# Whole weight pieces of two k pairs with joint extra sums, seven of eight pairs in the attention, and raw buffers handed out by stage

## The chip, the cores and the metric

The kernel runs on one core of a Trainium2 chip. The metric is the device time of one execution in microseconds (us). The core has a matmul engine (PE, with its weight loads shown as PEld), a vector engine (DVE), an activation engine (ACT), and SP, whose in-order queue issues the DMA transfers. Every engine takes its own instructions strictly in the order of the program.

## What is computed

Two layers on a sequence of 512 rows of 2048 numbers, both with RMS norms before and after and with shift, scale and gate from a conditioning vector. The first layer is an mLSTM with 8 heads, the second an attention with 16 heads whose keys and values come from one shared projection of the stream between the layers. All of it is float32.

```python
proj = h @ w_in                                   # mLSTM: queries/keys, values, two gates o and z
qk = silu(causal_conv(proj[..., :A_V0], ...))
ht = mlstm_chunkwise(heads(q), heads(k), heads(v), li, lf)
y = sigmoid(o) * rmsnorm(ht) * silu(z) @ w_out

kv = hkv @ kv_w                                   # shared keys and values
qz = h @ w_in                                     # attention: queries and gate
s = einsum(q, k) * scale + bias                   # chunk attends to itself and eight before it
y = einsum(softmax(s), v) * silu(z) @ w_out
x = x + gate * rmsnorm(y, g_post)                 # after each layer
```

## The kernel before

**Products.** Every operand is split in two parts, hi (rounded) and lo (the rest), and a product is three matmuls, hi by hi, lo by hi and hi by lo (`mm3`, through `mm`, L213). Weights are packed on the host in the order in which they are used (`stream`), and come as pieces of up to 128 x 1024 numbers. `wpiece` (L183 on) fetches one into a `raw` tile (L194, tile names wr), makes the extra sums if the piece has any (ws, L199 to L201), casts hi on ACT (wh, L179), subtracts lo on DVE (wl, L180), and splits the sums in the same way (wsh, wsl). `raw`, `hi` and `lo` have three buffers each in the pool `wp`.

**Two ways of multiplying.** `proj_s` makes two tiles of output columns together. Over a pair of k tiles it either does the ordinary products (`eight`: twelve matmuls of 512 columns) or a fast 2 x 2 scheme (`seven`: seven products, twenty-one matmuls of 256 columns), which needs sums of the weights (the ws tiles) and of the activations (`half_sums`, `three_sums`). `f` of the eight pairs go the fast way: 5 in heads 4 to 7 of the mLSTM, 6 to 8 in the keys, 6 in the attention. Its four sums stand in the PSUM tiles ps_d, ps_c, ps_a and ps_b and are combined by DVE.

**Order.** The tile scheduler places the instructions of each engine in one order at build time. Weights run ahead of the rest by a priority lead (`AHEAD`), and buffers decide how far. The stages are: adaLN and gates (to about 243 us), mLSTM heads 0 to 3, heads 4 to 7 (to about 1545), the first output product in rows (to about 1890; its first column group also reloads the stored gates as yr tiles through the raw buffers), the values' first half, the keys, the values' second half (to about 2240), the attention's heads (to about 2650), and the second output product. In both output products the last column group, and in the values the first half, runs as two halves of two row tiles each (`PAIRS`).

**Head 4.** At h == HALF the pools of the first half are closed, and the activation sums for the fast products (`head_sums`) are made there, five pairs of them.

**Attention.** A head's weights come in six pieces. In the middle of a head's projection, `mid` puts the mixing of the head before the last (ps_o, gated in L1021) and the scores and transposes of the last one (ps_s, ps_t) into PE's order. `fetch` loads a head's keys and values into one tile at the start of the head before.

**Residual.** `residual(m)` loads a row tile, adds the first layer's output and stores it; for rows 2 and 3 this stands at high priority, just ahead of the values.

Of the kernel before, what the change touches and what calls it, by code (L numbers as in the profile page):

```python
# [15 lines left out]
P = 128  # L16
# [16 lines left out]
AHEAD = 300  # L33

# [8 lines left out]
HEAD_PAIRS = 5  # L43
HALF = NH // 2
ATT_PAIRS = 6


def pair_pieces(f, step=1):


    sk, nk = list(range(f)), list(range(f, KT // 2))
    n = min(len(sk), len(nk))
    out = [([a], [b]) for a, b in zip(sk, nk)]
    out[1:1] = [([], nk[i : i + 2]) for i in range(n, len(nk), 2)]
    return out + [(sk[i : i + step], []) for i in range(n, len(sk), step)]


def stream():

    out = []  # L60

    def add(mat, kts, cs):
        out.append((mat, [(k, c, n) for k in kts for c, n in cs]))

    def tile_a(mat, col, kts=KT):
        for k in range(0, kts, 8):
# [6 lines left out]
    def tile_s(mat, c1, c2, f, step=1):  # L73
        for sk, nk in pair_pieces(f, step):
            blocks = [(2 * k + i, c, P) for i, c in ((0, c1), (0, c2), (1, c2), (1, c1)) for k in sk]
            out.append((mat, blocks + [(2 * k + i, c, P) for k in nk for i in range(2) for c in (c1, c2)]))

    for k0, k1 in BLOCKS:
        for k in range(k0, k1):
            add("a_w_in", [k], [(c, P) for c in LEAD])  # L80
        for c in LATER:
            add("a_w_in", range(k0, k1), [(c, P)])
    for h in range(NH):
        for c in (h * DK, V0 // 2 + h * DK):
            if 1 < h <= HALF:
                tile_a("a_w_in", c)
                tile_a("a_w_in", c + P)
            elif h > HALF:
                tile_s("a_w_in", c, c + P, HEAD_PAIRS)
        tile_b("a_w_in", V0 + h * DV)  # L90
        if h >= HALF:
            for i in range(4):
                tile_s("a_w_in", O0 + h * DV + i * P, Z0 + h * DV + i * P, HEAD_PAIRS)
        elif h:
            for c0 in (O0, Z0):
                for i in range(4):
                    tile_a("a_w_in", c0 + h * DV + i * P)
    tile_b("a_w_out", 0, 32)
    for _ in PAIRS:
        for g in range(1, 4):  # L100
            tile_b("a_w_out", g * 512, 32)
    for _ in PAIRS:
        for g in range(2):
            tile_b("kv_w", D + g * 512)
    for i in range(KT // 2):
        tile_s("kv_w", 2 * i * P, (2 * i + 1) * P, KEY_PAIRS[i], 2)
    for g in range(2, 4):
        tile_b("kv_w", D + g * 512)
    for h in range(BH):
        tile_s("b_w_in", h * P, D + h * P, ATT_PAIRS)  # L110
# [20 lines left out]
def hybrid_trunk(ctx, tc, xT, xN, c, adaT, cols, wst, wg, ext, kc, out):  # L131
# [50 lines left out]
    ahead = [0]  # L182

    def wpiece(mat, ns=0, pl=None, bufs=2):


        i, at = wpos
        m, blocks = order[i]
        assert m == mat
        n = sum(w for _, _, w in blocks)  # L190
        wpos[:] = i + 1, at + P * n
        with tc.high_priority(ahead[0]):
            raw = wp.tile([P, 1024], F32, tag="raw", name=f"wr{i}")[:, :n]
            nc.sync.dma_start(raw, wst[at : at + P * n].rearrange("(p n) -> p n", p=P))  # L194
            out = []
            if ns:
                w = ns * P
                t = pl.tile([P, 3 * w], F32, tag="ws", name=f"ws{i}", bufs=2)
                nc.vector.tensor_tensor(t[:, : 2 * w], raw[:, w : 3 * w], raw[:, : 2 * w], op=ALU.subtract)  # L199
                nc.vector.tensor_tensor(raw[:, w : 2 * w], t[:, w : 2 * w], raw[:, :w], op=ALU.add)  # L200
                nc.vector.tensor_tensor(t[:, 2 * w :], raw[:, 3 * w : 4 * w], raw[:, w : 2 * w], op=ALU.subtract)  # L201
# [3 lines left out]
            if ns:  # L205
                sh = pl.tile([P, 3 * w], F32R, tag="wsh", name=f"wsh{i}", bufs=bufs)
                sl = pl.tile([P, 3 * w], F32R, tag="wsl", name=f"wsl{i}", bufs=bufs)
                split(sh, sl, t)
                return hi, lo, sh, sl
        return hi, lo  # L210
# [9 lines left out]
    def proj(mat, xs, pss, nk, k0, k1, last, t0=0, t1=S, first=None):  # L220

        g = len(pss)
        for ka in range(k0, k1, nk):
            hi, lo = wpiece(mat)
# [9 lines left out]
    def proj_b(mat, xs, pss, ms=range(4), kts=KT, at={}, late=0):  # L234
# [3 lines left out]
        for k0 in range(0, kts, 2):  # L238
            if k0 in at:
                at[k0]()  # L240
            held.append((k0, *wpiece(mat)))
# [13 lines left out]
    def proj_s(mat, xs, ss, f, z1, z2, name, pl, bufs, at={}, step=1):  # L255
# [3 lines left out]
        pieces = pair_pieces(f, step)  # L259
        begun = set()  # L260
        h0, h1_ = slice(0, 256), slice(256, 512)
        for i, (sk, nk) in enumerate(pieces):
            if i in at:
                at[i]()
            ns = len(sk)
            parts = wpiece(mat, ns, pl, bufs)

            def acc(ps, cols, b, x, last):
                start = id(ps) not in begun
                begun.add(id(ps))  # L270
                hi, lo = parts[:2] if b >= 0 else parts[2:]
                w0 = (b if b >= 0 else b + 3 * ns) * P
                w = slice(w0, w0 + P)
                mm3(ps[:, cols], hi[:, w], lo[:, w], x[:, 0, :], x[:, 1, :], start, last)

            def eight():
                for m, k in enumerate(nk):
                    for j in range(2):
                        for t, ps in enumerate((A, B)):
                            acc(ps, slice(0, S), 4 * ns + 4 * m + 2 * j + t, xs[2 * k + j], False)  # L280

            def seven():
                end = i == len(pieces) - 1
                for ps, cols, b0, x, last in (
                    (D, h1_, ns, lambda k: ss[k][1], False),
                    (D, h0, 0, lambda k: xs[2 * k][:, :, h0], end),
                    (C, h0, -2 * ns, lambda k: ss[k][2], False),
                    (C, h1_, -3 * ns, lambda k: ss[k][0], end),
                    (A, h0, 3 * ns, lambda k: xs[2 * k + 1][:, :, h0], False),
                    (A, h1_, -ns, lambda k: xs[2 * k + 1][:, :, h1_], end),  # L290
                    (B, h0, 2 * ns, lambda k: ss[k][3], end),
                ):
                    if i == 0 and ps is B:
                        eight()
                    for j, k in enumerate(sk):
                        acc(ps, cols, b0 + j, x(k), last and j == ns - 1)
# [3 lines left out]
            seven()  # L300
# [60 lines left out]
    sp = st.enter_context(pool("start"))  # L361
# [100 lines left out]
    bp = mst.enter_context(pool("ada1", side="right"))  # L462
# [110 lines left out]
    def pair(c, name):  # L573
        z1, z2 = (acp.tile([P, 2, 256], F32, tag="so", name=f"{name}_{i}", bufs=6) for i in range(2))
        proj_s("a_w_in", h1, h1s, HEAD_PAIRS, z1, z2, name, hq, 2)
# [32 lines left out]
    for h in range(NH):  # L608
# [49 lines left out]
        if h == HALF:  # L658
            head_sums()
# [87 lines left out]
    rp = rst.enter_context(pool("rp", bufs=12, side="right"))  # L747
# [3 lines left out]
    def y_tile(k):  # L751
        while len(ys) <= k:
            h, q = divmod(len(ys) // 2, 2)
            with tc.high_priority(AHEAD):
                raw = wp.tile([P, 2, S], F32, tag="raw", name=f"yr{h}_{q}")
# [144 lines left out]
    with tc.high_priority(AHEAD):  # L900
        residual(2)
        residual(3)
    for pair, ms in enumerate(PAIRS):
        for g in range(2):
# [3 lines left out]
            values(g, ms, turn)  # L908
    rst.close()
    zst = ExitStack()  # L910
    zp = zst.enter_context(pool("zp", bufs=2, side="right"))
    for i in range(KT // 2):
# [4 lines left out]
        proj_s("kv_w", hkv, hs, ready, z[:, 0:2, :], z[:, 2:4, :], f"k{i}", zp, 2, at, 2)  # L917
# [9 lines left out]
    for k in range(0, KT, 2):  # L927
# [11 lines left out]
        for i in range(2):  # L939
            split(h2[k + i][:, 0, :], h2[k + i][:, 1, :], raw[i])  # L940
    zst.close()
# [4 lines left out]
    kv = []  # L946

    def fetch(h):
        t = kq.tile([P, 2, S], F32, tag="kv", name=f"kv{h}", bufs=3)
        nc.sync.dma_start(t[:, 0, :], ksc[h // 2][:, h % 2, :])  # L950
        nc.sync.dma_start(t[:, 1, :], vsc[h // 4][:, h % 4, :])
        kv.append(t)

    fetch(0)

    def queries(h, mid):

        if h < BH - 1:
            fetch(h + 1)
        z = at.tile([P, 4, 256], F32, tag="z", name=f"z{h}", bufs=2)  # L960
        proj_s("b_w_in", h2, h2s, ATT_PAIRS, z[:, 0:2, :], z[:, 2:4, :], f"z{h}", kq, 3, {3: mid})
# [7 lines left out]
        split(k[:, 0, :], k[:, 1, :], kv[h][:, 0, :])  # L969
        bias = at.tile([P, S], F32, tag="b", name=f"bias{h}", bufs=2)  # L970
# [5 lines left out]
    def weights(h, q0, q, k, bias):  # L976
# [3 lines left out]
        for i in range(4):  # L980
            n = P * (i + 1)
            ps = newa(f"ps_s{h}_{i}")
            if i == 0:
                mm(ps[:, :n], q0, kv[h][:, 0, :P], True, True)
# [12 lines left out]
    def flipped(h, pr):  # L997
# [14 lines left out]
        split(v[:, 0, :], v[:, 1, :], kv[h][:, 1, :384])  # L1012
        return pts, v

    def mixed(h, pts, v, sz):
# [4 lines left out]
        mm(ps[:, 384:], kv[h][:, 1, 384:], pts[3], False, True)  # L1020
# [122 lines left out]
```

## Time and profile before

| | |
|---|---|
| median of 3 runs | 2827.09 us (2824.44 to 2833.84) |
| the profiled execution | 2828.65 us, span 2826.9 us, mean clock of PE 0.997 |
| PE, PEld, DVE, ACT busy | 99%, 86%, 73%, 47% of the span |
| matmuls on PE | 15173 |
| weight loads (wr) | 466 of 512 KB, 138 of 256 KB, 16 of 384 KB |

The span is the stretch that the profiler covers; the profiled execution's own time is 1.75 us longer. Busy time on PE is not speed: matmuls overlap, and the length listed for one includes its tail. Idle time is given with what ended it, so a wait names its releaser. The granted clock is the share of full speed that PE was given.

### The profile page before, as it was taken

The numbers are of one execution on the slowest core, as the hardware profiler recorded it, in microseconds if no ns is written. First come the engines' busy times: TensorE is split into PE (matmuls) and PEld (weight loads), VectorE is DVE, ScalarE is ACT, GpSimd is POOL, SyncE is SP. The second block draws the span as 40 slices with busy tenths as digits, with TensorE's granted clock in tenths as the row PEclk, the third lists the DMA queues.
The fourth block names the chain that finished last, engine by engine and source line by source line (L and its number), as shares of the span: only waits on it lengthen the run. The fifth ranks groups of instructions, "written<-read, shape, count | busy, mean of one in ns | idle before, by whom it ended". The sixth has DMA issues, their size and how long they took to land.

```text
span 2826.9 us, 40577 instructions
## 1 busy us (share of the span) xinstructions
PE 2788.7 (99%) x15173; PEld 2417.6 (86%) x15173; DVE 2050.1 (73%) x3668; ACT 1337.0 (47%) x2040; POOL 0.2 (0%) x4
## 2 busy tenths in 40 slices
PE   7999999999999999999999999999999999999998
PEld 5787888888888989989888888888998899999887
DVE  7986978878688776766857445567985688888625
ACT  4234524234234554544635344468534466666523
POOL 0000000000000000000000000000000000000000
PEclk9999999999999999999999999999999999999999
DMA  8875687878774332332323656788535534334634
GB/s 296 300 256 179 230 313 237 298 237 282 263 245 136 98 125 85 105 105 97 116 86 135 217 198 212 251 264 283 176 130 186 157 120 128 118 126 124 222 110 171
DMA packets 184606, 524.09 MB, mean 185 GB/s; under 512 B 19620, under 2 KB 37060, under 8 KB 183896
## 3 DMA queue, kind: packets, MB, share of 16 engines
q1 hardware_dynamic: 184408, 521.49, 55.1%
q8 instruction: 119, 1.95, 0.3%
q14 instruction: 79, 0.65, 0.1%
HBM read 487.81 MB, written 38.85 MB: 186 GB/s over the span
## 4 chain that ended last, share of the span: by engine, by line
PE 89%; DVE 4%; DMA 3%; ACT 2%; issue 1%; SPq 0%; DVEq 0%; ACTq 0%
PE ps_y L213 17%; PE ps_v L213 10%; PE ps_o L213 6%; PE ps_z L213 5%; PE ps_azo L213 4%; PE ps_qk L213 4%; PE ps_az L213 4%; PE ps_kv L213 4%; PE ps_l L213 3%; PE ps_bzo L213 3%; PE ps_bz L213 3%; PE ps_dz L213 2%; PE ps_cz L213 2%; PE ps_s L213 2%; PE ps_czo L213 2%; PE ps_dzo L213 2%
## 5 line engine op out<-in xcount | busy, mean ns | idle before, releaser
L179 ACT CAST wh<-wr 128x1024 fp32r<-128x1024 f32 (+3 forms) x640 | 595.8, 932 | 833.3 <-PE ps_y L213 230.3
L180 DVE TENSOR_TENSOR wl<-wr,wh 128x1024 fp32r<-128x1024 f32 (+3 forms) x640 | 687.4, 1075 | 390.2 <-ACT wh L179 384.3
L213 PE MATMUL ps_y<-wh,y 128*128 128x512 f32 x1536 | 475.9, 390 | 0.0
L213 PEld LDWEIGHTS ps_y<-wh,y 128*128 128x128 f32 x1536 | 288.3, 188 | 59.3
L213 PE MATMUL ps_v<-wh,h 128*128 128x512 f32 x1024 | 321.7, 390 | 0.0
L179 ACT CAST wsh<-ws 128x384 fp32r<-128x384 f32 (+1 forms) x238 | 131.1, 551 | 356.3 <-issue 171.1
L213 PE MATMUL ps_y<-wl,y 128*128 128x512 f32 x768 | 299.3, 390 | 0.0
L180 DVE TENSOR_TENSOR wsl<-ws,wsh 128x384 fp32r<-128x384 f32 (+1 forms) x238 | 143.3, 603 | 154.1 <-ACT wsh L179 154.0
L213 PEld LDWEIGHTS ps_v<-wh,h 128*128 128x128 f32 x1024 | 192.3, 188 | 40.3 <-DVE zq L306 0.9
L213 PE MATMUL ps_v<-wl,h 128*128 128x512 f32 x512 | 199.9, 390 | 0.0
L370 DVE CUSTOM_DVE_ANT_0 ada<-ada,scB,cl 128x1024 f32<-128x1024 f32 x128 | 163.9, 1281 | 23.4 <-DMA ada<-in_adaT 23.2
L370 DVE CUSTOM_DVE_ANT_0 ada<-ada,scB,mod 128x1024 f32<-128x1024 f32 x128 | 164.0, 1281 | 21.6 <-DMA ada<-in_adaT 20.1
L213 PEld LDWEIGHTS ps_y<-wl,y 128*128 128x128 f32 x768 | 144.2, 188 | 29.9 <-DVE wl L180 0.5
L213 PE MATMUL ps_kv<-wh,hkv 128*128 128x512 f32 x512 | 160.6, 393 | 1.0 <-ACT wh L179 1.0
L199 DVE TENSOR_TENSOR ws<-wr 128x256 f32<-128x256 f32 (+1 forms) x238 | 106.1, 452 | 35.3 <-DMA wr<-in_wst 34.1
L213 PE MATMUL ps_qk<-h,wh 128*128 128x512 f32 x384 | 119.1, 390 | 0.0
L213 PE MATMUL ps_o<-h,wh 128*128 128x512 f32 x384 | 118.3, 389 | 0.0
L213 PE MATMUL ps_z<-h,wh 128*128 128x512 f32 x384 | 118.2, 389 | 0.0
L213 PEld LDWEIGHTS ps_kv<-wh,hkv 128*128 128x128 f32 x512 | 96.6, 189 | 21.1 <-ACT wh L179 1.4
L213 PEld LDWEIGHTS ps_v<-wl,h 128*128 128x128 f32 x512 | 96.2, 188 | 19.7 <-issue 0.9
L213 PE MATMUL ps_l<-h,wh 128*128 128x512 f32 x320 | 99.1, 391 | 2.5 <-ACT oz L456 2.0
L213 PE MATMUL ps_kv<-wl,hkv 128*128 128x512 f32 x256 | 100.6, 393 | 0.8 <-DVE wl L180 0.8
(385 smaller groups left out, 5865.3 us busy)
## 6 DMA issues: line engine op xcount, KB each, us to landing
wr<-in_wst SPq DMA_DIRECT2D x466, 512.0 KB, 4.0
ada<-in_adaT SPq DMA_DIRECT2D x256, 512.0 KB, 5.9
wr<-in_wst SPq DMA_DIRECT2D x138, 256.0 KB, 2.7
xt<-nsc SPq DMA_DIRECT2D x44, 256.0 KB, 4.1
yr<-ysc SPq DMA_DIRECT2D x16, 512.0 KB, 4.3
wr<-in_wst SPq DMA_DIRECT2D x16, 384.0 KB, 5.4
bsc<-in_ext SPq DMA_DIRECT2D x16, 320.0 KB, 5.7
xt<-in_xT SPq DMA_DIRECT2D x4, 1024.0 KB, 7.1
```

What stands on the lines that cost most here:

```text
L179: nc.scalar.copy(hi, src)
L180: nc.vector.tensor_tensor(lo, src, hi.bitcast(F32), op=ALU.subtract)
L199: nc.vector.tensor_tensor(t[:, : 2 * w], raw[:, w : 3 * w], raw[:, : 2 * w], op=ALU.subtract)
L213: nc.tensor.matmul(ps, a, b, start=start, stop=stop)
L370: pin(nc.vector.tensor_tensor_reduce(at, at, scB[:, j * D // 2 : (j + 1) * D // 2], 1.0, mod[:, i : i + 1] if j else col(CB + i), ALU.mult ...
```

## The change

1. `raw` tiles: the pool `wp` keeps two instead of three buffers (`RAW_BUFS`). A third, for each third piece, is lent by a pool of the stage (`spare`): at the start, in heads 0 to 3, in the first output product's pool `rp` (used through the first half of the values), and in the keys. In heads 4 to 7, in the second half of the values, in the attention and in the second output product there is none. Of the reloaded y2r tiles, the first two use `wp`, the others a pool of their own.
2. `pair_pieces`: a piece with extra sums is always whole. Those that hold two fast pairs have either joint sums (`merged`, in keys and attention: sums of 512, 256, 256 columns and a split of 768) or two separate sets (heads 4 to 7).
3. The attention makes 7 of 8 pairs the fast way. A head has four pieces of 1024; `mid` stands before the third one. The split sums wsh and wsl have two buffers instead of three. Keys and values have tiles of their own, fetched in `mid`; the bias tile has one buffer instead of two.
4. Head 4's first column pair makes 4 pairs the fast way (`RAMP`), and the fifth pair's activation sums are made at its second piece.
5. `residual(2)` and `residual(3)` lose their high priority.

Over the kernel, PE gets 315 more matmuls of 256 columns and 180 fewer of 512, and SP issues 54 fewer loads for the same bytes.

```diff
+RAW_BUFS = 2
+RAMP = [4, 5, 5, 5]
-ATT_PAIRS = 6
-def pair_pieces(f, step=1):
+ATT_PAIRS = 7
+def pair_pieces(f, merged=False):
     sk, nk = list(range(f)), list(range(f, KT // 2))
-    n = min(len(sk), len(nk))
-    out = [([a], [b]) for a, b in zip(sk, nk)]
-    out[1:1] = [([], nk[i : i + 2]) for i in range(n, len(nk), 2)]
-    return out + [(sk[i : i + step], []) for i in range(n, len(sk), step)]
+    n = len(nk)
+    assert n <= f
+    out = [([[a]], [b]) for a, b in zip(sk, nk)]
+    return out + [([sk[i : i + 2]] if merged else [[k] for k in sk[i : i + 2]], []) for i in range(n, f, 2)]
...
-    def wpiece(mat, ns=0, pl=None, bufs=2):
+    def wpiece(mat, groups=(), pl=None, bufs=(2, 2)):
...
-            raw = wp.tile([P, 1024], F32, tag="raw", name=f"wr{i}")[:, :n]
+            own = spare[0] and i % (RAW_BUFS + 1) == 0
+            raw = (spare[0] if own else wp).tile([P, 1024], F32, tag="raw", name=f"wr{i}", bufs=1 if own else RAW_BUFS)[:, :n]
...
-            if ns:
+            for j, ns in enumerate(groups):
                 w = ns * P
...
-    sp = st.enter_context(pool("start"))
+    sp = spare[0] = st.enter_context(pool("start"))
...
-    bp = mst.enter_context(pool("ada1", side="right"))
+    bp = spare[0] = mst.enter_context(pool("ada1", side="right"))
...
             while loaded or pending:
                 background(3)
+            spare[0] = None
             mst.close()
...
-        if h == HALF:
-            head_sums()
...
-                o, sz = pair_oz = pair(O0 + h * DV + i * P, f"zo{h}_{i}")
+                f = HEAD_PAIRS if h > HALF else RAMP[i]
+                o, sz = pair(O0 + h * DV + i * P, f"zo{h}_{i}", f, {1: head_sums} if len(h1s) == f < HEAD_PAIRS else {})
...
-    rp = rst.enter_context(pool("rp", bufs=12, side="right"))
+    rp = spare[0] = rst.enter_context(pool("rp", bufs=12, side="right"))
...
-    with tc.high_priority(AHEAD):
-        residual(2)
-        residual(3)
+    residual(2)
+    residual(3)
...
+    spare[0] = None
     rst.close()
...
-        proj_s("kv_w", hkv, hs, ready, z[:, 0:2, :], z[:, 2:4, :], f"k{i}", zp, 2, at, 2)
+        spare[0] = zp
+        proj_s("kv_w", hkv, hs, ready, z[:, 0:2, :], z[:, 2:4, :], f"k{i}", zp, (2, 2), at, True)
...
-        proj_s("b_w_in", h2, h2s, ATT_PAIRS, z[:, 0:2, :], z[:, 2:4, :], f"z{h}", kq, 3, {3: mid})
+        proj_s("b_w_in", h2, h2s, ATT_PAIRS, z[:, 0:2, :], z[:, 2:4, :], f"z{h}", kq, (2, 2), {2: mid}, True)
...
-        bias = at.tile([P, S], F32, tag="b", name=f"bias{h}", bufs=2)
+        bias = at.tile([P, S], F32, tag="b", name=f"bias{h}")
...
             if 0 < h <= BH:
                 pr.extend(weights(h - 1, *qs.pop(h - 1)))
+            if h < BH - 1:
+                fetch_k(h + 1)
+            if h < BH:
+                fetch_v(h)
...
-            raw = wp.tile([P, 2, S], F32, tag="raw", name=f"y2r{i}")
+            raw = wp.tile([P, 2, S], F32, tag="raw", name=f"y2r{i}", bufs=RAW_BUFS) if i < 2 else op.tile([P, 2, S], F32, tag="yr", name=f"y2r{i}", bufs=2)
```

More of the change, by code (lines that the diff above doesn't have):

```diff
@@ L71, in tile_b, with tile_s @@
             add(mat, [k, k + 1], [(col, 512)])
-    def tile_s(mat, c1, c2, f, step=1):
-        for sk, nk in pair_pieces(f, step):
-            blocks = [(2 * k + i, c, P) for i, c in ((0, c1), (0, c2), (1, c2), (1, c1)) for k in sk]
+    def tile_s(mat, c1, c2, f, merged=False):
+        for sk, nk in pair_pieces(f, merged):
+            blocks = [(2 * k + i, c, P) for ks in sk for i, c in ((0, c1), (0, c2), (1, c2), (1, c1)) for k in ks]
             out.append((mat, blocks + [(2 * k + i, c, P) for k in nk for i in range(2) for c in (c1, c2)]))
@@ L92, in stream @@
             for i in range(4):
-                tile_s("a_w_in", O0 + h * DV + i * P, Z0 + h * DV + i * P, HEAD_PAIRS)
+                tile_s("a_w_in", O0 + h * DV + i * P, Z0 + h * DV + i * P, HEAD_PAIRS if h > HALF else RAMP[i])
         elif h:
@@ L182, in hybrid_trunk @@
     ahead = [0]
-    def wpiece(mat, ns=0, pl=None, bufs=2):
+    spare = [None]
+    def wpiece(mat, groups=(), pl=None, bufs=(2, 2)):
         i, at = wpos
@@ L192, in wpiece @@
         with tc.high_priority(ahead[0]):
-            raw = wp.tile([P, 1024], F32, tag="raw", name=f"wr{i}")[:, :n]
+            own = spare[0] and i % (RAW_BUFS + 1) == 0
+            raw = (spare[0] if own else wp).tile([P, 1024], F32, tag="raw", name=f"wr{i}", bufs=1 if own else RAW_BUFS)[:, :n]
             nc.sync.dma_start(raw, wst[at : at + P * n].rearrange("(p n) -> p n", p=P))
-            out = []
-            if ns:
+            ts = []
+            c0 = 0
+            for j, ns in enumerate(groups):
                 w = ns * P
[L198 to L201, printed above, removed]
+                r = raw[:, c0 : c0 + 4 * w]
+                t = pl.tile([P, 3 * w], F32, tag="ws", name=f"ws{i}_{j}", bufs=bufs[0])
+                nc.vector.tensor_tensor(t[:, : 2 * w], r[:, w : 3 * w], r[:, : 2 * w], op=ALU.subtract)
+                nc.vector.tensor_tensor(r[:, w : 2 * w], t[:, w : 2 * w], r[:, :w], op=ALU.add)
+                nc.vector.tensor_tensor(t[:, 2 * w :], r[:, 3 * w :], r[:, w : 2 * w], op=ALU.subtract)
+                ts.append(t)
+                c0 += 4 * w
             hi = wp.tile([P, 1024], F32R, tag="hi", name=f"wh{i}")[:, :n]
@@ L204, in wpiece @@
             split(hi, lo, raw)
-            if ns:
-                sh = pl.tile([P, 3 * w], F32R, tag="wsh", name=f"wsh{i}", bufs=bufs)
-                sl = pl.tile([P, 3 * w], F32R, tag="wsl", name=f"wsl{i}", bufs=bufs)
+            out = [(hi, lo)]
+            for j, t in enumerate(ts):
+                sh = pl.tile(list(t.shape), F32R, tag="wsh", name=f"wsh{i}_{j}", bufs=bufs[1])
+                sl = pl.tile(list(t.shape), F32R, tag="wsl", name=f"wsl{i}_{j}", bufs=bufs[1])
                 split(sh, sl, t)
-                return hi, lo, sh, sl
-        return hi, lo
+                out.append((sh, sl))
+        return out
     def mm(ps, a, b, start, stop):
@@ L253, in proj_b, with proj_s @@
             held.clear()
-    def proj_s(mat, xs, ss, f, z1, z2, name, pl, bufs, at={}, step=1):
+    def proj_s(mat, xs, ss, f, z1, z2, name, pl, bufs, at={}, merged=False):
         D, C, A, B = [newp(f"ps_{n}{name}") for n in "dcab"]
-        pieces = pair_pieces(f, step)
+        pieces = pair_pieces(f, merged)
         begun = set()
@@ L264, in proj_s, with acc @@
                 at[i]()
-            ns = len(sk)
-            parts = wpiece(mat, ns, pl, bufs)
-            def acc(ps, cols, b, x, last):
+            main, *extra = wpiece(mat, [len(ks) for ks in sk], pl, bufs)
+            def acc(ps, cols, parts, b, x, last):
                 start = id(ps) not in begun
                 begun.add(id(ps))
[L271 to L274, printed above, removed]
+                w = slice(b * P, (b + 1) * P)
+                mm3(ps[:, cols], parts[0][:, w], parts[1][:, w], x[:, 0, :], x[:, 1, :], start, last)
             def eight():
+                b0 = 4 * sum(len(ks) for ks in sk)
                 for m, k in enumerate(nk):
@@ L279, in eight, with seven @@
                         for t, ps in enumerate((A, B)):
[L280 to L291, printed above, removed]
+                            acc(ps, slice(0, S), main, b0 + 4 * m + 2 * j + t, xs[2 * k + j], False)
+            def seven(g, ks):
+                ns = len(ks)
+                b0 = 4 * sum(len(u) for u in sk[:g])
+                end = i == len(pieces) - 1 and g == len(sk) - 1
+                for ps, cols, t, at_, x, last in (
+                    (D, h1_, 0, 1, lambda k: ss[k][1], False),
+                    (D, h0, 0, 0, lambda k: xs[2 * k][:, :, h0], end),
+                    (C, h0, 1, 1, lambda k: ss[k][2], False),
+                    (C, h1_, 1, 0, lambda k: ss[k][0], end),
+                    (A, h0, 0, 3, lambda k: xs[2 * k + 1][:, :, h0], False),
+                    (A, h1_, 1, 2, lambda k: xs[2 * k + 1][:, :, h1_], end),
+                    (B, h0, 0, 2, lambda k: ss[k][3], end),
                 ):
-                    if i == 0 and ps is B:
+                    if i == 0 and g == 0 and ps is B:
                         eight()
-                    for j, k in enumerate(sk):
-                        acc(ps, cols, b0 + j, x(k), last and j == ns - 1)
+                    for j, k in enumerate(ks):
+                        acc(ps, cols, extra[g] if t else main, (0 if t else b0) + at_ * ns + j, x(k), last and j == ns - 1)
             if i:
                 eight()
-            seven()
+            for g, ks in enumerate(sk):
+                seven(g, ks)
         with tc.high_priority(AHEAD):
@@ L754, in y_tile @@
             with tc.high_priority(AHEAD):
-                raw = wp.tile([P, 2, S], F32, tag="raw", name=f"yr{h}_{q}")
+                raw = wp.tile([P, 2, S], F32, tag="raw", name=f"yr{h}_{q}", bufs=RAW_BUFS)
                 nc.sync.dma_start(raw, ysc[h, :, 2 * q : 2 * q + 2, :])
@@ L940, in hybrid_trunk @@
             split(h2[k + i][:, 0, :], h2[k + i][:, 1, :], raw[i])
+    spare[0] = None
     zst.close()
@@ L945, in hybrid_trunk, with fetch, fetch_k, fetch_v @@
     at = ast.enter_context(pool("att"))
[L946 to L954, printed above, removed]
+    kt, vt = [], []
+    def fetch(h, ts, src, tag):
+        ts.append(at.tile([P, S], F32, tag=tag, name=f"{tag}{h}", bufs=2))
+        nc.sync.dma_start(ts[h], src)
+    def fetch_k(h):
+        fetch(h, kt, ksc[h // 2][:, h % 2, :], "kt")
+    def fetch_v(h):
+        fetch(h, vt, vsc[h // 4][:, h % 4, :], "vt")
+    fetch_k(0)
     def queries(h, mid):
-        if h < BH - 1:
-            fetch(h + 1)
         z = at.tile([P, 4, 256], F32, tag="z", name=f"z{h}", bufs=2)
-        proj_s("b_w_in", h2, h2s, ATT_PAIRS, z[:, 0:2, :], z[:, 2:4, :], f"z{h}", kq, 3, {3: mid})
+        proj_s("b_w_in", h2, h2s, ATT_PAIRS, z[:, 0:2, :], z[:, 2:4, :], f"z{h}", kq, (2, 2), {2: mid}, True)
         qz = z.rearrange("p a t -> p (a t)")
@@ L968, in queries @@
         k = at.tile([P, 2, S], F32R, tag="kk", name=f"k{h}")
[L969 to L970 removed]
+        split(k[:, 0, :], k[:, 1, :], kt[h])
+        bias = at.tile([P, S], F32, tag="b", name=f"bias{h}")
         b0 = bsc[h]
@@ L1011, in flipped @@
         v = at.tile([P, 2, 384], F32R, tag="vv", name=f"vv{h}")
-        split(v[:, 0, :], v[:, 1, :], kv[h][:, 1, :384])
+        split(v[:, 0, :], v[:, 1, :], vt[h][:, :384])
         return pts, v
```

16 lines of the change are left out of this document (8 added, 8 removed).

## Prediction

> **What bounds the kernel now.** I read the page first, then the waits of the matmul engine, then single stages. The page gives the shares and the chain of work that ended last:
> ```profile
> PE 2788.7 (99%) x15173; PEld 2417.6 (86%) x15173; DVE 2050.1 (73%) x3668; ACT 1337.0 (47%) x2040; POOL 0.2 (0%) x4
> PE 89%; DVE 4%; DMA 3%; ACT 2%; issue 1%; SPq 0%; DVEq 0%; ACTq 0%
> ```
> PE is busy for 99% of the span. A gain can therefore come from cheaper products or from the few stops of PE, and from nothing else. The stops between 100 and 2810 us, longest first (waiter, what ended the wait, us, times, longest):
> ```profile
> PE ps_dzo L213 <- ACT wh L179: 3.7, 1, 3.7
> PE ps_kv L213 <- ACT wh L179: 1.0, 1, 1.0
> ...
> PE ps_kv L213 <- DVE wl L180: 0.8, 1, 0.8
> ```
> The first is at 895, where head 4 begins its joint columns; the others are at 1904, early in the values. Busy time and granted clock around them, and in a steady stretch of the attention:
> ```profile
> 895.00:900.00 5.00, 1.27 (x5) 1.14 (x5) 5.00 (x11) 3.68 (x6) 0.00 (x0) 0.72 0.16 52
> 900.00:905.00 5.00, 5.00 (x21) 4.43 (x20) 3.49 (x9) 1.51 (x3) 0.00 (x0) 0.59 0.30 108
> 1905.00:1910.00 5.00, 3.35 (x9) 2.42 (x10) 2.61 (x4) 2.75 (x4) 0.00 (x0) 0.76 0.82 251
> 2400.00:2450.00 50.00, 49.97 (x357) 46.77 (x356) 43.08 (x117) 32.42 (x63) 0.00 (x0) 1.00 0.39 123
> ```
> After the length come PE, PEld, DVE, ACT and POOL, then the clock, DMA share and GB/s. A stop costs its idle time and then a low clock: 0.59 over 900 to 905 is 5 x 0.41 = 2.05 us more, so the first stop costs 5.8 us. The stop at 1904 shows 0.76 after only 1.74 us of idleness; I put its low clock at 0.8 us on top, 2.5 us in all. By the Trainium skill, page "TensorE: Matmul & The Clock Gate", Part 1, the clock falls only after an idle window of about 3.4 us; by that rule the second stop would cost 1.7 us. The first stop agrees with the rule, the 0.76 at the second does not, and the row is used. In the attention nothing is free: PE 49.97 of 50, DVE 43.08, so heads cost what PE costs, with DVE not far behind.
>
> **Products.** One k pair of an attention head, ordinary and then fast, in the timeline of PE (start, length, tile):
> ```profile
> 2408.33 0.63 PE L213 MATMUL ps_az<-h,wh 128*128 128x512 f32 x2
> ...
> 2411.08 0.40 PE L213 MATMUL ps_bz<-h2s,wh 128*128 128x256 f32 x2
> ...
> 2414.57 0.40 PE L213 MATMUL ps_dz<-h2s,wh 128*128 128x256 f32 x2
> ...
> 2417.08 0.40 PE L213 MATMUL ps_dz<-h2s,wh 128*128 128x256 f32 x2
> ```
> Twelve 512-wide matmuls take 2411.08 - 2408.33 = 2.75 us, twenty-one 256-wide ones 2417.08 - 2414.57 = 2.51 us. Listed lengths (0.28 to 0.39) contain a tail that overlaps, so starts are the price. A pair turned from ordinary to fast saves 0.24 us. Sixteen heads get one more fast pair and the first column pair of head 4 one fewer: 15 x 0.24 = **-3.6 us**. The same page of the Trainium skill (Part 1, on the 2.5 ns) has N / 2.4 GHz + 2.5 ns a matmul, as an estimate 0.295 us a pair and -4.4 us; the trace is slower on both widths (0.229 and 0.120 us), so its row is used.
>
> **Joint pieces and extra sums.** The attention's weights come as four full pieces a head instead of two full and four half ones. Prices on DVE, from the groups by form in 2350 to 2600 (line, tile, shape, busy, mean ns):
> ```profile
> L180 DVE TENSOR_TENSOR wsl<-ws,wsh 128x384 fp32r<-128x384 f32 x60 | 33.3, 555 | 20.9 <-ACT wsh L179 20.9
> L180 DVE TENSOR_TENSOR wl<-wr,wh 128x512 fp32r<-128x512 f32 x40 | 27.5, 688 | 0.0
> L199 DVE TENSOR_TENSOR ws<-wr 128x256 f32<-128x256 f32 x59 | 24.6, 417 | 0.5 <-DMA wr<-in_wst 0.5
> L180 DVE TENSOR_TENSOR wl<-wr,wh 128x1024 fp32r<-128x1024 f32 x20 | 24.4, 1222 | 7.1 <-ACT wh L179 7.1
> ```
> Before, a head needs 6 x (0.417 + 0.285 + 0.288 + 0.555) + 4 x 0.688 + 2 x 1.222 = 14.5 us of weight work on DVE. After: one piece with a single pair, 1.545 + 1.222 = 2.8, and three joint pieces of 512, 256, 256 and 768 columns; I price those 0.69, 0.42, 0.42 and 0.96 by the slope of the rows, 3.7 us with the 1.22, so 13.9 in all. DVE and ACT lie under PE, so this brings no time by itself; 54 fewer issues of 0.33 us on SP bring none either, as the bytes are the same. Keys and values fetched apart, in the middle of a head, add one DMA queue step per head before the weights' loads: nothing while loads lead by a piece. The bias has one buffer instead of two, so its load waits until the last scores have read it; the weights behind it in SP's queue wait longer for their own buffer, so that adds nothing.
>
> The room for the attention's split sums falls from three to two. DVE takes its instructions in order, so a subtraction of sums that waits for room holds what is queued behind it: the gate product that reads ps_o (L1021) and frees PE's third score tile. I walked one head by these durations. From the head's first matmul, the room comes free at 9.4 us, its subtraction ends at 11.2, that of the fourth piece at 12.5, the first sum of the next head at 13.1, the gate product at 13.8; PE wants the bank at about 14.1. A margin of 0.3 us is within what the walk can tell, so I charge 0.06 us a head, **+1.0 us** (0 to +5).
>
> **Head 4.** One pair's activation sums leave the front. From the weights' subtraction at 873.05 to v's first, DVE then has 4 x 1.14 + 14 x 0.60 + 6 x 0.47 + 17 x 0.334 + 7 x 0.205 = 22.9 us in its queue (1024, 512, 384, 256, 128 columns, start to start), while PE has 893.44 - 873.05 = 20.4 us and 0.7 more before it needs the first split sums: still 1.8 us late, and by the same count 1.0 us at the next tile. What is late next is again DVE. 2.8 us of idleness instead of 3.7, in two shorter stops: **-1.5 us** (0, if the clock falls as much, to -5.8, if both vanish).
>
> **Values.** At 1904 the weights of the values stand in SP's queue behind the row loads and stores of the last residual rows, which now lose their precedence. Weights go first: **-2.5 us** (0 to -3.4, with the whole clock deficit of 1905 to 1915).
>
> **Two raw buffers instead of three.** Where a spare is lent (rows in halves, first values, keys) there are three as before. In heads 4 to 7 and in the attention PE spends at least 5 us on a piece, and two buffers deliver one per 3 to 3.5 us; that is hidden. In the output rows of the first layer five loads pass for three pieces of 5.45 us, 16.35 us of PE against 5 x 3.3 = 16.5 us: hidden by the lead of several us at its start, with little left. The last column group of the second output product is different: 16 pieces, each for two row tiles. In ACT's timeline, PE releases one cast after another there:
> ```profile
> 2776.42 1.05 ACT L179 CAST wh<-wr 128x1024 fp32r<-128x1024 f32 x1 [1.02 <-PE ps_y L213]
> 2779.14 1.05 ACT L179 CAST wh<-wr 128x1024 fp32r<-128x1024 f32 x1 [1.67 <-PE ps_y L213]
> ```
> In DVE's, the subtraction that frees the raw buffer of the first of them; and in the raw tile's own group, from 2745 on, the landing:
> ```profile
> 2777.51 1.23 DVE L180 TENSOR_TENSOR wl<-wr,wh 128x1024 fp32r<-128x1024 f32 x1 [1.45 <-ACT wh L179]
> ```
> ```profile
> DMA to landing us min/median/max: 3.1/3.4/5.4
> ```
> PE eats a piece per 2.72 us. A raw buffer is taken for 3.4 (landing) + 2.3 (cast to the end of the subtraction) + 0.2 (handovers) = 5.9 to 6.0 us, so two give a piece per 3.0 us. Counted from 2773.7, where the group starts, piece 4 is issued at 2.4 and piece 5 at 5.1; six periods later 14 and 15 are ready at 38.3 and 41.0, or 43 with the last landing of 5.4. Their use is at 36.7 and 38.1. The early lead covers the rest, the end does not: **+4.0 us** (0 to +6).
>
> Sum: -3.6 + 1.0 - 1.5 - 2.5 + 4.0 = -2.6 us. The profiled execution took 2828.65 us (1.75 around the span), so 2826.0; it stands 1.56 above the median of the runs, so about 2824.5. About 0.3%, 8.5 us, is what a measurement of this kernel tells from no change; the forecast is within it.
>
> **Rivals.** First, the stops go and nothing new comes: -3.6 - 5.8 - 3.4 = -12.8, or 2814. For it: each of these stops is named by the change. Against: DVE is full from 880 to 895, and the last group's arithmetic. Chance 0.2.
>
> Second, slower: two raw buffers throttle the attention. The first sum of the next head's second piece stands in DVE's queue right ahead of the gate product; its load can start only when the piece two before it is split, at 8.0 us of the head, and DVE wants it at 12.5. It decides above a landing of about 4.4 us. The page has 4.0 for such loads, the end of the kernel up to 5.4, and each us over the mark stops PE in all 16 heads: at 5.4, 16 us, or 2840. Against: DMA is at 0.39 here. Chance 0.25.
>
> Third, the products save nothing, because weight loads bind as in the key stage, where every product is 256 wide and PEld is busy for all of the time: the sum is +1.0, about 2828. Against: the 0.120 us above are just as large there. Chance 0.1.
>
> **Numbers.** Forecast 0.45 at 2824.5, rivals 0.2, 0.25 and 0.1. Faster by over 0.3% comes from the first rival, 0.2; slower from the second and a little of the forecast's own tail, 0.28; the rest is 0.52. The range takes in the first rival and the second almost to its full price: 2813 to 2839.
>
> **What would show it.** Right: about 25.2 instead of 25.4 us from one ps_o to the next; a shorter stop at ps_czo near 893; no stop at ps_kv near 1904; 3 to 5 us of waits of ps_y for wh or wl after 2800. Wrong: repeated waits of ps_s for L1036's product or of ps_t in the attention, casts that wait for wr there, stops of ps_y in the 1515 to 1700 stretch, or an end without waits.

## The result, and the profile after

The changed kernel takes 2833.47 us in the median of 12 runs, the kernel before 2825.98 in the same runs. The ratio is 1.0026, with a 95% interval of 1.0017 to 1.0035: 7.5 us slower, where the sum had 2.6 us faster. The time lies inside the stated range, on the other side of no change.

The page's shares and the chain that ended last:

```profile
PE 2788.1 (98%) x15308; PEld 2421.5 (85%) x15308; DVE 2057.1 (73%) x3488; ACT 1333.3 (47%) x1957; POOL 0.2 (0%) x4
PE 85%; DVE 7%; DMA 4%; ACT 2%; issue 2%; SPq 0%; DVEq 0%; ACTq 0%
```

PE is as busy as before, in a longer span; DVE has a larger part of the chain. The five longest waits of PE between 100 and 2815 us (waiter, what ended the wait, us, times, longest):

```profile
PE ps_czo L223 <- DVE v L182: 3.0, 1, 3.0
PE ps_t L1018 <- DVE pt L182: 2.7, 5, 1.1
PE ps_y L223 <- ACT wh L181: 2.3, 1, 2.3
PE ps_s L223 <- DVE e L605: 1.1, 1, 1.1
PE ps_azo L223 <- DVE v L182: 1.0, 1, 1.0
```

The two stops of ps_kv are gone. In place of one stop of 3.7 us at head 4 there are two of 3.0 and 1.0. New are five waits of ps_t in the attention, and a stop of ps_y at 2811. The windows with the clock:

```profile
1905.00:1910.00 5.00, 5.00 (x24) 4.14 (x23) 3.64 (x4) 3.62 (x7) 0.00 (x0) 1.00 0.99 333
2400.00:2450.00 50.00, 49.75 (x376) 47.62 (x375) 43.80 (x100) 32.23 (x55) 0.00 (x0) 1.00 0.38 127
2815.00:2820.00 5.00, 5.00 (x16) 4.01 (x17) 1.23 (x1) 1.04 (x1) 0.00 (x0) 0.67 0.02 9
```

1904 is now at full clock; 2815 to 2820, behind the new stop, is at 0.67.

A ledger shows where the time went. It takes the start of the first matmul of a tile in PE's timeline, and compares the length from one such start to the next, so that early differences don't carry on:

| stretch, from the first matmul of ... to ... | before | after | difference |
|---|---|---|---|
| start to ps_dzo (head 4) | 893.44 | 894.32 | +0.9 |
| ps_dzo to ps_y (heads 4 to 7) | 638.94 | 637.42 | -1.5 |
| ps_y to ps_kv (first output rows) | 356.05 | 356.45 | +0.4 |
| ps_kv to ps_dk (values) | 94.95 | 91.15 | -3.8 |
| ps_dk to ps_dz (keys, values) | 251.41 | 251.85 | +0.4 |
| ps_dz to the last ps_o (attention) | 417.19 | 420.39 | +3.2 |
| last ps_o to PE's end (second output rows) | 165.52 | 171.28 | +5.8 |
| PE's end to the end of the span | 9.40 | 10.74 | +1.3 |

The sum is +6.7 us, the difference of the spans. In 13 steady heads one ps_o follows the other after 25.50 us before and 25.67 after. Forecast was 25.2.

The ledger compares one trace with one trace, and its stretches vary from trace to trace. The traces of the experiments below that leave a stretch's code as it is in the changed kernel give 891.9 to 894.9 us to ps_dzo, 636.6 to 638.9 for heads 4 to 7, 91.0 to 93.5 for the values, 25.64 to 25.75 for a head and 169.2 to 172.8 for the end (without att_single7, whose last ps_o stands elsewhere). Only the values, the attention, the end and the tail differ by more than such a spread.

### The profile page after: what moved, and what is told of

It reads as the page before. It is cut to its first block, busy times and chain, and to the rows that moved or that the text cites. A ratio compares the mean times of both kernels' runs of the same rounds, so it can differ in the third digit from the quotient of the medians.

```text
span 2833.6 us, 40474 instructions
## 1 busy us (share of the span) xinstructions
PE 2788.1 (98%) x15308; PEld 2421.5 (85%) x15308; DVE 2057.1 (73%) x3488; ACT 1333.3 (47%) x1957; POOL 0.2 (0%) x4
## 4 chain that ended last, share of the span: by engine, by line
PE 85%; DVE 7%; DMA 4%; ACT 2%; issue 2%; SPq 0%; DVEq 0%; ACTq 0%
PE ps_y L223 16%; PE ps_v L223 10%; PE ps_o L223 6%; PE ps_z L223 5%; PE ps_azo L223 4%; PE ps_qk L223 4%; PE ps_kv L223 4%; PE ps_bzo L223 3%; PE ps_l L223 3%; PE ps_az L223 3%; PE ps_cz L223 2%; PE ps_dz L223 2%; PE ps_s L223 2%; PE ps_czo L223 2%; PE ps_dzo L223 2%; DVE wl L182 2%
## 5 line engine op out<-in xcount | busy, mean ns | idle before, releaser
L181 ACT CAST wh<-wr 128x1024 fp32r<-128x1024 f32 (+3 forms) x586 | 585.0, 999 | 824.9 <-PE ps_y L223 201.5
L182 DVE TENSOR_TENSOR wl<-wr,wh 128x1024 fp32r<-128x1024 f32 (+3 forms) x586 | 678.4, 1159 | 396.2 <-ACT wh L181 395.0
```

Source lines behind the costliest of these rows:

```text
L181: nc.scalar.copy(hi, src)
L182: nc.vector.tensor_tensor(lo, src, hi.bitcast(F32), op=ALU.subtract)
```

## Experiments

Each edit is to the changed kernel unless it says otherwise. Ratios are to the kernel before, with the 95% interval; "a head" is the mean step from one ps_o to the next over the same 13 heads. The runs were taken in three groups, in which the kernel before took 2828.01, 2826.19 and 2827.32 us, so ratios compare better than microseconds.

### The attention's wait

What ps_t waits for is seen in one head. Before, in DVE's timeline and then PE's:

```profile
2437.65 0.69 DVE L180 TENSOR_TENSOR pt<-ps_t,pt 128x512 fp32r<-128x512 f32 x1
```
```profile
2438.49 0.27 PE L1003 MATMUL ps_t<-kcs,s 128*128 128x128 f32 x1
```

After, the worst head, DVE and then PE:

```profile
2507.25 0.95 DVE L182 TENSOR_TENSOR wsl<-ws,wsh 128x768 fp32r<-128x768 f32 x1
2508.12 1.22 DVE L182 TENSOR_TENSOR wl<-wr,wh 128x1024 fp32r<-128x1024 f32 x1
2509.25 0.68 DVE L206 TENSOR_TENSOR ws<-wr 128x512 f32<-128x512 f32 x1
...
2510.31 0.95 DVE L182 TENSOR_TENSOR wsl<-ws,wsh 128x768 fp32r<-128x768 f32 x1
...
2511.99 1.15 DVE L182 TENSOR_TENSOR pt<-ps_t,pt 128x512 fp32r<-128x512 f32 x2
```
```profile
2512.82 0.30 PE L1018 MATMUL ps_t<-kcs,s 128*128 128x128 f32 x1 [1.13 <-DVE pt L182]
```

A head transposes four score tiles into ps_t. The fourth takes the PSUM bank of the first, and that is free only when DVE has split tile 0 into pt. DVE does this behind four wide weight operations of 0.68 to 1.22 us. In PE's order the fourth transpose has six 512-wide matmuls fewer and four 256-wide ones more ahead of it than before, by the rows 6 x 0.227 - 4 x 0.120 = 0.9 us less. So PE comes sooner, DVE doesn't, and PE stands.

Nine of the 14 heads show no such wait in the list of waits, and still lose. After, in a head without a listed one:

```profile
2434.94 0.28 PE L223 MATMUL ps_dz<-h2s,wh 128*128 128x256 f32 x1
2435.29 0.30 PE L1018 MATMUL ps_t<-kcs,s 128*128 128x128 f32 x1
```

The starts are 0.35 us apart where the pace is 0.12. The listed length of 0.28 hides the gap, so it isn't idle time. Gaps have to be read from starts. Read so, the fourth transpose costs 0.40 us a head over 14 heads: 0.23 in every head, and 0.17 more on average from the five listed waits.

Those five have a second cause. Item 3 of the change also takes one of the bias tile's two buffers. What DVE waited for the bias between 2300 and 2620, and the longest of these waits, in the worst head:

```profile
DVE bias L988 <- DMA bias<-bsc: 6.4, 6, 1.8
```
```profile
2502.08 0.11 DVE L988 MEMSET bias<- 64x64 f32 x1 [1.79 <-DMA bias<-bsc]
```

Before, DVE never waits for the bias there: the load is issued 16 us ahead of DVE's memset of the tile. After, it is issued only when DVE has read the only buffer for the last scores, and the memset follows 3.3 to 5.1 us later. A late load holds DVE's queue: the 1.79 us above are idle time of DVE. The five listed waits stand in the heads with DVE's five longest bias waits, in the same order of length: 0.83, 1.01, 1.14, 1.21 and 1.79 us for the bias, and 0.46, 0.63, 0.76, 0.83 and 1.41 us from start to start at the fourth transpose. No run gives the bias its second buffer back, so this share is read from the trace and not measured by an edit.

**pt_first** puts the split of tile 0 at the weights' priority.

```diff
-                split(t[:, 0, :], t[:, 1, :], ps[:, :n])
+                with tc.high_priority(AHEAD if j == 0 else 0):
+                    split(t[:, 0, :], t[:, 1, :], ps[:, :n])
```

> The changed kernel with one edit: the split of the first transposed tile (pt0) stands at the weights' priority, so DVE takes it third after a head's evacuation instead of ninth. Theory A (the attention lost its gain because the fourth transpose, ps_t, waits for DVE's split of pt0, which frees its PSUM bank, behind the wider weight splits): the waits of ps_t for pt go, ps_o to ps_o falls from 25.67 to about 25.3 to 25.45 us, the kernel from 2833.5 to 2828.5 to 2831. Theory B (two raw buffers or two split-sum buffers pace the attention): no gain, 2833 or more, since the weights' splits only come later. Theory C (a seventh fast pair is simply worth nothing next to narrow transposes and scores): waits go, but a head stays at 25.45 to 25.5.

Measured: 2829.69 us, ratio 1.0004 (0.9996 to 1.0013), a head 25.34. What is left of the wait between 100 and 2840:

```profile
PE ps_t L1018 <- DVE pt L182: 1.1, 2, 0.7
```

A gain of 0.33 us a head, as theory A had it. Theory B had no gain, and theory C a head at 25.45 or more; both are missed. The two waits that are left stand behind DVE's two longest bias waits in this trace, 1.19 and 1.48 us; eleven of the 13 heads take 25.2 to 25.3 us.

**t3_end3.** This leaves DVE's order in a head as it is in the changed kernel and changes which bank the last transpose needs. It also has the repair of the last column group (below).

```diff
-        pts = []
-        for j in range(4):
+        pts = [None] * 4
+        for j in (3, 0, 1, 2):
...
+                with tc.high_priority(-15 if j == 2 else 0):
                     nc.tensor.transpose(...)
...
+                with tc.high_priority(60):
                     nc.scalar.copy(t, ps[:, :n])
-            pts.append(t)
+            pts[j] = t
...
+        spare[0] = rp if g == 3 else None
```

> The changed kernel with the third raw buffer in the last column group, and the transposes in the order 3, 0, 1, 2. The last transposed tile then needs the bank that ACT's short copy of tile 3 frees (early in ACT's order), not the bank that DVE's split of tile 0 frees; the order of DVE's instructions in a head is that of the changed kernel. Theory A (the bank held by DVE's late split is what the attention lost): waits of ps_t for DVE go although nothing was done for DVE, a head at 25.25 to 25.35 us, the kernel at 2822 to 2824. Rival (the split at higher priority helped by relieving the rest of DVE's queue): a head stays at 25.6 to 25.75, the kernel at 2827 to 2828.

Measured: 2824.29 us, ratio 0.9988 (0.9979 to 0.9996), a head 25.28, as theory A had it; the kernel is 0.3 us above its range. It is the lowest ratio of all, just clear of the kernel before, though not of pt_end3 below. DVE's and then PE's timeline:

```profile
2435.73 1.15 DVE L182 TENSOR_TENSOR pt<-ps_t,pt 128x512 fp32r<-128x512 f32 x2
```
```profile
2431.64 0.27 PE L1019 MATMUL ps_t<-kcs,s 128*128 128x128 f32 x1
```

DVE's split of tile 0 is as late as ever, and DVE still waits for the bias (4.6 us in 6 waits between 2300 and 2620), but the last transposes are on PE four us before the split. So it was the bank, and not the load of DVE's queue. PE then is busy for all of the same window:

```profile
2400.00:2450.00 50.00, 50.00 (x380) 48.23 (x379) 44.46 (x100) 32.00 (x57) 0.00 (x0) 1.00 0.39 127
```

**att_six** (`ATT_PAIRS = 6`) and **pt_six** (the same with pt_first's edit) price the seventh pair.

> The changed kernel with six instead of seven fast pairs in the attention, still as four whole pieces with joint sums. Theory A: ps_t's waits shrink, because the second piece holds an ordinary pair and less sum work, and the wide matmuls cover the transpose: a head at 25.4 to 25.5 us, the kernel at 2829 to 2832. Theory B (buffers): the pieces and buffers are the same, so it stays at 2833 to 2834. If the pair's price of 0.24 us held and no wait changed, it would be 2837.

Measured: 2833.13 us, ratio 1.0023 (1.0013 to 1.0033), a head 25.63. Neither expectation was met in full. The kernel is no faster than with seven pairs, but the wait did shrink, as theory A had it: in 11 of 14 heads the fourth transpose starts 0.23 to 0.24 us after a 512-wide matmul, which is the pace, and most heads take about 25.48 us. Two heads still lose 0.94 us each, behind two bias waits of 1.63 us. What the shorter wait gives back, the missing pair takes.

> The changed kernel with pt0's split at the weights' priority and six instead of seven fast pairs. It prices the seventh pair where no wait covers it. By the rows 0.24 us a head: ps_o to ps_o at 25.55 to 25.6 us against 25.34, the kernel at 2833 to 2834. If the seventh pair is worth nothing next to narrow transposes: 25.34, 2829 to 2830.

Measured: 2831.44 us, ratio 1.0019 (1.0010 to 1.0028), a head 25.55 against pt_first's 25.34. The seventh pair is worth 0.22 us a head where no wait covers it, close to the row's 0.24; the most common step falls by 0.24, from 25.45 to 25.21. The third rival falls.

**Buffers.** Six pairs leave room for one more buffer of either kind.

```diff
 six_raw3:
-    at = ast.enter_context(pool("att"))
+    at = spare[0] = ast.enter_context(pool("att"))
 six_wsh3:
-        proj_s(..., f"z{h}", kq, (2, 2), {2: mid}, True)
+        proj_s(..., f"z{h}", kq, (2, 3), {2: mid}, True)
```

> Six fast pairs with joint pieces (as att_six) and a third raw buffer in the attention. Theory A: within 0.1 us a head of att_six's 25.63, 2832 to 2834. Theory B' (two raw buffers pace the attention, the second rival of the prediction): 25.4 or less, 2829.

Measured: 2841.85 us, ratio 1.0048 (1.0035 to 1.0061), a head 25.58, within 0.1 of att_six. Raw buffers do not pace the steady attention, and the second rival of the prediction falls; in the changed kernel's own trace, too, DVE waits for no weight load between 2300 and 2620. The kernel is slower for another reason: PE stops once for 4.4 us before the steady heads, which fits a lent buffer in a pool that opens only with the attention. Waits from 2220 on:

```profile
PE ps_az L223 <- ACT wh L181: 4.4, 1, 4.4
...
PE ps_t L1018 <- DVE pt L182: 0.8, 1, 0.8
```

> Six fast pairs with joint pieces (as att_six, which leaves the room) and three instead of two buffers for the split sums. Theory A: order of DVE counts, not this room; within 0.1 us a head of att_six's 25.63, the kernel at 2832 to 2834. Theory B (the room for split sums paces DVE): 25.4 or less, 2829.

Measured: 2847.52 us, ratio 1.0070 (1.0057 to 1.0082), a head 26.48. Theory B falls, and theory A's "within 0.1" as well, in a telling direction:

```profile
PE ps_t L1018 <- DVE pt L182: 9.7, 14, 1.4
```

In the order as built, the split of tile 0 is the eighth of DVE's instructions from a head's last evacuation on. In six_raw3, with two such buffers, it is the fourth. More room let weight work move ahead of it, and PE waits longer: 0.34 to 1.82 us from start to start at the fourth transpose, over the pace in every head. The bias is not the cause here; DVE waits for it once, 0.23 us at the end.

**att_single7** goes back to single pairs in half pieces, with seven fast pairs, three split-sum buffers and `mid` before the fourth piece.

> The changed kernel with seven fast pairs in the attention, but single pairs in pieces of half size with their own sums, three split-sum buffers and the mixing before the fourth piece, as the kernel before had them; raw buffers stay at two. Theory A says the wide blocks of joint sums delay DVE's split of tile 0: here the blocks are half as long, though DVE has about 1 us more work a head. A head at 25.3 to 25.5 us, the kernel at 2829 to 2831. Rival (the two raw buffers hold the attention): 25.65 or more, 2833 or more, since half pieces need twice the loads through the same two buffers.

Measured: 2847.01 us, ratio 1.0072 (1.0059 to 1.0084), a head 25.96. Theory A's number is missed and the rival's direction met, but not its cause alone: the three longest listed waits from 2220 on are ps_t for pt (3.9 us, 11 times), ps_s for the gate product of ps_o (2.3, 3 times) and ps_s for mx (1.8, once), all on DVE. DVE in turn waited for loads between 2300 and 2620, 5.1 us for the bias and 2.2 us for weights. Which part of the loss is DVE's extra work, which the order and which these loads stays open.

### The end

The stop of the last column group, in PE's timeline, and the landing times of wr from 2745 on:

```profile
2813.64 0.72 PE L223 MATMUL ps_y<-wh,y 128*128 128x512 f32 x2 [2.35 <-ACT wh L181]
```
```profile
DMA to landing us min/median/max: 3.1/3.3/6.6
```

The load that the stop waits for is the one of 6.6 us, issued at 2805.8.

**end_raw3** lends a buffer from the stage's x2 pool for the whole second output product.

```diff
     rp = ost.enter_context(pool("x2", bufs=8))
+    spare[0] = rp
```

> The changed kernel with a third raw buffer in the second output product (lent by that stage's x2 pool). Theory A (the last column group starves on two buffers): the stop of 2.3 us of ps_y near 2812 and the low clock behind it go, 4.5 to 6.5 us less, 2827 to 2829. Rival (the last loads land late only because the output rows are stored at the same time): the stop stays at over 1.5 us, 2831 to 2833.

Measured: 2849.03 us, ratio 1.0075 (1.0063 to 1.0088). A miss for both. My reading is that the stage's pool takes the room of the attention's, so that a load into it waits until the attention is over. The first ps_y starts at 2659.2 instead of 2634.9, with a wait of 5.9 us there. The only other listed wait of ps_y is one of 0.3 us, so the stop near 2812 did go; the total can't show it.

**end_last3** lends it for the last column group alone, where the pool has long been open.

```diff
     for g in range(4):
         gate_row(1, g)
+        spare[0] = rp if g == 3 else None
```

> The changed kernel with a third raw buffer for the last column group of the second output product only, from a pool that is already open by then. Theory A (that group starves on two buffers): no stop of ps_y near 2812, no low clock behind it, 4.5 to 5.5 us less than the changed kernel: 2828 to 2829. Rival (late loads by the output's stores): the stop remains, 2832 to 2834.

Measured: 2827.44 us, ratio 1.0007 (0.9998 to 1.0016). From the last ps_o to PE's end 165.42 us instead of 171.28, as long as before (165.52); all that is left of waits from 2660 on:

```profile
PE ps_y L223 <- DVE wl L182: 0.2, 1, 0.2
```

The last two weight loads are issued at 2800.2 and 2801.4 instead of 2805.8 and 2809.8, and the last one still takes 6.4 us to land. So a slow landing alone makes no stop; together with the late issue it does. What makes it slow isn't shown.

The tail goes back too, 9.56 instead of 10.74 us. The chain of work, before the change and then after it, shows where the tail came from:

```profile
2815.62 2.74 DVE yo L1071 x4
2818.36 0.61 DVE yo L771
```
```profile
2822.90 0.69 DVE yo L782
...
2823.70 2.74 DVE yo L1090 x4
```

Before, the third row tile is finished (four products, 2.74 us) ahead of the last evacuation, mostly under PE's last matmuls, which end at 2817.5. After, the evacuation stands first in DVE's order, and both row tiles are finished after PE's end at 2822.9. In end_last3 the order is again that of before.

**pt_end3** joins pt_first and end_last3.

> Both repairs together: the split of pt0 at the weights' priority, and the third raw buffer in the last column group. If the two losses are independent, the gains add: 3.8 + 5 us under the changed kernel, 2824 to 2826, about 2 to 4 us below the kernel before. If the attention's gain had only moved its wait to the output rows, it is 2828 or more.

Measured: 2823.97 us, ratio 0.9994 (0.9985 to 1.0003), a head 25.40, the end 165.16: both gains are there. By the ratios, the two alone would add up to 0.9985, the edge of the interval.

### The two repairs of the change

**res_first** puts `residual(2)` and `residual(3)` at high priority again.

> The changed kernel with the last two residual rows at high priority again, as before the change. Theory A (their precedence made the stop at 1904): waits of ps_kv of 1.5 to 2 us with a lower clock come back, +3.4 us, 2836 to 2838. Rival (the stop went because of the other buffers): no change, 2833 to 2834.

Measured: 2838.42 us, ratio 1.0034 (1.0022 to 1.0047). From ps_kv to ps_dk it takes 94.99 us against 91.15 after and 94.95 before, and two waits of ps_kv come back (1.3 us together); the low clock doesn't, it is 1.00 from 1900 to 1920. The twelve traces without the precedence take 91.0 to 93.5 us, so it costs 1.5 to 4 us. The direction is shown by these traces, the size of 3.8 is not, and the ratio's interval overlaps that of the changed kernel.

**ramp_five** has `RAMP = [5, 5, 5, 5]` and calls `head_sums()` before the first column pair of head 4 again.

> The changed kernel with five fast pairs from head 4's first column pair on, and all activation sums before it, as before the change. By the ledger of the two traces the ramp gained 1.5 us between the first ps_dzo and the first ps_y: the stop at the head's start goes back to 3.5 to 4 us and the kernel to 2834.5 to 2835.5. Rival (the ramp does nothing, the order is DVE's anyway): 2833 to 2834.

Measured: 2833.91 us, ratio 1.0027 (1.0016 to 1.0038), no slower than the changed kernel. The waits from 880 to 915:

```profile
PE ps_dzo L223 <- ACT wh L181: 3.3, 1, 3.3
PE ps_dzo L223 <- DVE wl L182: 0.3, 1, 0.3
```

Its heads 4 to 7 take 637.50 us against 637.42. The ramp turns one stop of 3.6 us into two of 4.0 together and gains nothing. The 1.5 us of the ledger in this stretch are no more than the spread of this stretch between traces, 636.6 to 638.9 us.

## Why the prediction was wrong

**The failing step is the attention.** The price of a pair was right: 0.24 us forecast, 0.22 measured between pt_six and pt_first. The walk of one head was wrong. It followed the split-sum room to the gate product of ps_o and PE's third score tile, found a margin of 0.3 us there, and charged 1.0 us. That place held: no wait of ps_s for this product is listed after. The walk left out the bank of the fourth transpose, which pt_first and t3_end3 show to be the wait. The durations of the prediction and the order as built would have led there: from the head's first matmul, the split of tile 0 ends near 6 us on DVE, and the 25 narrow and 12 wide matmuls ahead of the fourth transpose take 25 x 0.120 + 12 x 0.227 = 5.7 us on PE. And it put the bias tile's single buffer at nothing, looking only at the weights behind that load in SP's queue; but DVE has to wait for the load too, and the trace shows 6.4 us of it. The wait at the transpose costs 25.67 - 25.28 = 0.39 us a head, by the starts 0.23 from the order and 0.17 behind the late bias; that is more than the pair saves. Together the attention is +3.2 us where 16 x (0.06 - 0.24) = -2.9 was forecast: 6.1 of the 9.3 us between the two sums.

**The end** was right in kind and undersized: a stop on the third raw buffer's account, 4.0 us forecast, 5.8 measured to PE's end and 1.3 more in the tail, whose order on DVE the forecast left out. The other traces with this end have 3.7 to 7.3 us to PE's end, so what the forecast surely lacked is the tail. The walk by 6.0 us a buffer gave pieces 14 and 15 late by 1.6 to 4.9 us, with a last landing of up to 5.4 where it took 6.6; the wait was 2.35 + 0.30 us, and a clock of 0.67 over 5 us made 1.65 more of it.

By the Trainium skill, page "TensorE: Matmul & The Clock Gate", Part 1, the array's clock drops after an idle window of about 3.4 us. The trace differs here: idle stretches of 2.35 and 0.30 us went with a granted clock of 0.67 in the 5 us from 2815.

**The values** were right in direction, -2.5 forecast and -3.8 measured in one pair of traces. By res_first and the spread of this stretch the edit is worth 1.5 to 4 us, so the size of the forecast fits as well.

**Head 4** was right in kind and wrong in size. Two stops on DVE were forecast, 1.8 and 1.0 us; 3.0 and 1.0 came, no less than the one stop of 3.7 before, and ramp_five shows that the ramp is worth nothing.

**The other raw buffers** were right: no stop in the first output rows or in heads 4 to 7 on a load, and six_raw3 leaves the attention's step as it was. One correction to the list of the change: by the kernel's code the keys' lent buffer stays in use through the values' second half, so there are three there as well.

## What to carry to other kernels

When work is taken off the engine that binds, everything behind it on that engine comes sooner; for each such instruction, look up which buffer or PSUM bank it reuses, and where in the other engine's queue the release stands. A short instruction that frees a bank, behind wide ones in an in-order queue, can be put ahead of them (pt_first) or made needless by another order (t3_end3); here both gave the loss back. A load into a tile with a single buffer can hold such a queue too, whatever else stands in it. And read gaps on a pipelined engine from start to start, since waits shorter than a listed tail don't show as idle time.

## What was not expected

More room can cost time: a third split-sum buffer made a head 26.48 instead of 25.63 us, because the order built with it puts more weight work ahead of what PE waits for. A buffer lent from a pool that opens late costs more than it gives: 14 us in the second output product (1.0075 against 1.0026 of 2826 us) and 4.4 us at the attention's start.
